# Four edits to the order of work in a two-layer backbone: a q tile's slot, gating written behind the next scores, a barrier behind a head's last scores, and spread roots in other PSUM banks

## The chip, the cores and the metric

The program runs on one core of one Trainium2 chip. The metric is the device time of one execution in microseconds (us), taken over several runs; lower is better. The core has five engines that each work through their own queue in order: TensorE (PE, matmuls; its weight loads are listed apart as PEld), VectorE (DVE), ScalarE (ACT), GpSimd (POOL) and SyncE (SP). In this kernel SP issues the loads from DRAM and POOL the stores to it.

## What is computed

Two layers over 512 latent tokens (x) and 256 context tokens, width 1024, batch 1. Layer 0 is a bidirectional multi-scale retention with 4 heads (q and k of 256 per head, v and a gate path z of 512 per head, rotary positions on q and k, a decay per head and direction); layer 1 is a chunked gMLP with a spatial gate. Each branch is gated by silu(z), projected, scaled by a gate from the conditioning vector, and added to x. Cut to what matters here:

```python
for i in range(DEPTH):                       # DEPTH = 2
    hx = rmsnorm(x, norm_g[i]) * (1 + scale_x) + shift_x
    hc = rmsnorm(ctx, norm_g[i]) * (1 + scale_c) + shift_c
    if i == 0:                               # retention, per head:
        s = (q @ k.T) * decay                # over context and latent keys, both directions
        o = s @ v
        o = o * rsqrt(mean(o * o) + eps)     # over the head's 512 columns
        out = (o * silu(z)) @ w_out
    else:                                    # gMLP
        u, v, z = hx @ w_in
        v = layernorm(v) * vnorm_g
        y = u * (w_s @ v_chunk + b_s)
        out = (y * silu(z)) @ w_out
    x = x + gate_x * out
return rmsnorm(x, final_g)
```

Everything is float32. The kernel writes each float32 operand of a matmul as a high and a low part and takes three products (low by high, high by low, high by high; `mm3`).

## The kernel before

**How an operand is split.** `split` casts on ScalarE (the high part) and subtracts on VectorE (the low part). Tiles that go through it appear in the profile under their names: `hl` (weights), `ph` and `pl` (scores), `qk`, `v`, `og` (the gated output of a head). Weights are first loaded as `raw` tiles.

**How weights are streamed.** `Stream` (`Q`) holds an ordered list of weight pieces. `pump` gives each load the first free slot of those it is allowed (w0 to w6 for the projections of layer 0) and `upto` makes the splits two pieces ahead of the product that uses them. Products over pairs of halves are arranged so that seven products do the work of eight: quads of raws 11, 12, 21, 22, with differences made on VectorE in place (`raw<-raw`). The last quad of layer 0's projections is `("vz", 3, 1)`, the one before it `("kq", 3)`.

**Layer 0.** The projections of all heads run first. Their results q, k (after `rope`), v and z go to DRAM through POOL and come back per head. `load_qk(h)` brings five tiles of a head (k, q, k, context k, q) into slots of SBUF and splits them; even and odd heads use different slots. `load_v(h)` does the same for v and z, `load_wo(h)` for the output weights, `decay(h)` for the head's decay table `dt`. These are generators: `aside` runs one step of one of them at a place written into the loops, and `step` runs one step of `background`, which reads the conditioning weights of the second layer (`ada_a` from `bg` tiles). The last of its four pieces uses the slots w2 and w3.

**A head, `attend`.** Six steps of scores (two halves of the queries, three pairs of key blocks). `score` makes the scores of a pair in a bank of the PSUM pool `tm` (two banks), multiplies them with the decay (`pf`, VectorE), and splits them (`ph` on ScalarE, `pl` on VectorE). `pv` multiplies scores with v two steps later (LAG = 2), into banks of the pool `ps` (six banks). After the last pair of a half `finish` takes the sums of squares and their root on ScalarE (`junk`, `ss`), the reciprocal on VectorE, and the gated rows `gt`; `flip` transposes them on TensorE and splits them into `og`. The flip of the first half stands at step 6 of the loop, between the P V products of scores 4 and 5 (counted from 0); the one of the second half inside the output projection, `project_out`.

**The turn to layer 1.** In the output projection of head 3 `prepare` starts the weight stream of layer 1 (`hl_e` is its first split, into a slot of its own), and the norm of the new x is taken: `by_tokens` transposes x into `ps` banks and sums squares, `inverse` makes the roots, `rms` spreads them over the partitions with four small matmuls into a PSUM bank and copies them to `rs`; `residual` copies the transposed x from its banks (`xs`). From `rs` follow the operands of layer 1, among them S1 (`oS`), which the third product, T1, needs.

**What sets the order.** TensorE's instructions keep the order of the text. On ScalarE, VectorE and the DMA queues a scheduler at build time may reorder, by data and by its own estimate of when things are ready, with text order as priority. The class `Queue` adds constraints: while `pinned` is set (inside `aside`), an instruction must follow the last one issued in the text on its engine; `kept` keeps all in order; `fence()` makes everything later in the text on that engine follow the last instruction issued before it:

```python
def fence(self):
    self.last = self.recent
```

A slot that is given out again is written only after its last reader. The functions that the change touches:

Of the kernel before, what the change touches and what calls it, by code (L numbers as in the profile page):

```python
# [10 lines left out]
ALU = mybir.AluOpType  # L11
AX = mybir.AxisListType

P = 128
# [12 lines left out]
HS = 256  # L27
# [40 lines left out]
def hybrid_kernel(ctx, tc, xT_d, cT_d, cv_d, sv_d, rows_d, ada0_d, adag_d, w_d, rope_d, dec_d, ws_d, id_d, out_d):  # L68
# [181 lines left out]
    for q in QUADS[3:]:  # L250
        Q.quad(q, SINGLE)
        for u in RAWS:
            Q.load((q, u), W, 1, parts_of(q, u))
    PROJECTED = len(Q.items)
    def place_at(tag):
        return lambda: st([P, 2, 1024], tag, F32R, name="hl_e")
# [506 lines left out]
    def background():  # L763
        for i in range(4):
            a = None
            for a in ada_piece(i, *(("g1", ("g2", "g3")) if i < 3 else ("oA22", ("w2", "w3")))):
                if a is None:
                    yield
            yield
            if i == 0:  # L770
                yield from columns(a, gate0)
                dve.tensor_tensor(gate0, gate0, gateb0, ALU.add)
            elif i == 1:
                yield from columns(a, sh1)
                dve.tensor_tensor(sh1, sh1, adab1[:, 0, :], ALU.add)
                dve.tensor_tensor(shs, sh1[:, 0:4], sh1[:, 4:8], ALU.add)
            elif i == 2:
                yield from columns(a, gs1)
                dve.tensor_tensor(gs1, gs1, adab1[:, 1, :], ALU.add)
                dve.scalar_tensor_tensor(gs1, gs1, 1.0, g1, ALU.add, ALU.mult)  # L780
            else:
                gb = st([P, D], "g1", name="gateb1")
                load(gb, rows_d[0:1, :].partition_broadcast(P))
                yield
                for j in range(2):
                    pr = pt(tag="tm")
                    mm(pr, ones, a[:, j * 512:j * 512 + 512], start=True, stop=True)
                    dve.tensor_tensor(gb[:, j * 512:j * 512 + 512], pr, gb[:, j * 512:j * 512 + 512], ALU.add)
                Q.gate = gb
            yield i  # L790
# [45 lines left out]
        dve.tensor_tensor(l, f32(l), f32(h), ALU.subtract)  # L836

    def load_qk(h):
        tags = ("s0", "s1", "s2", "s3", "rope") if h % 2 == 0 else ("w4", "w5", "g2", "g3", "w6")
        srcs = (k_d[h][0], q_d[h][0], k_d[h][1], kc_d[h], q_d[h][1])  # L840
        t = []
        for tag, src in zip(tags, srcs):
            t.append(st([P, 2, 2, HS], tag, F32R, name="qk"))
            load(f32(t[-1][:, 1]).rearrange("p a b -> p (a b)"), src)
            if len(t) % 2:
                yield
        for x in t:
            halves(x)
            yield
        qk[h] = (t[1], t[4]), (t[0], t[2]), t[3]  # L850
        yield
# [77 lines left out]
    def attend(h, qs, vs):  # L929
        q, k, kc = qk.pop(h)  # L930
        v, z = vv.pop(h)
        dt = dts[h]
        og = [st([P, 2, 4, HS], tag, F32R, name="og") for tag in ("oS3", "oS4")]
        steps = [(hf, j) for hf in range(2) for j in range(0, NK, 2)]
        ph, po, pend = {}, {}, []

        def key(j):
            return (k[j // 2], j % 2) if j < NT else (kc, j - NT)

        def score(hf, j):  # L940

            p = pt(tag="tm")
            for o in range(2):
                src, jj = key(j + 1 - o)
                for m in range(2):
                    l = (src[:, 0, m, jj * P:jj * P + P], src[:, 1, m, jj * P:jj * P + P])
                    mm3(p[:, o * HS:o * HS + HS], l, (q[hf][:, 0, m, :], q[hf][:, 1, m, :]), m == 0, m == 1)
            j1 = j + 1
            s0 = hf * HS - P * j1 + P * (NT - 1) if j < NT else XW + hf * HS - P * (j1 - NT) + P * (NC_T - 1)
            base = dt[:, s0:s0 + HS]  # L950
            both = bass.AP(base.tensor, base.offset, [base.ap[0], (P, 2), (1, HS)])
            two = lambda x: x.rearrange("p (o t) -> p o t", o=2)
            a = t2("pf")
            dve.scalar_tensor_tensor(two(a), two(p), 1.0 / 16.0, both, ALU.mult, ALU.mult)
            hl = t2("ph", dt=F32R), t2("pl", dt=F32R)
            split(hl, a)
            ph[hf, j] = hl

        def pv(hf, j):
            if j == 0:  # L960
                po[hf] = [pt(), pt()]
            h, l = ph.pop((hf, j))
            src = v[j // 2]
            for jj in range(2):
                for t in range(2):
                    o = (1 - jj) * HS + t * P
                    mm3(po[hf][t], (h[:, o:o + P], l[:, o:o + P]), (src[:, 0, jj, :], src[:, 1, jj, :]),
                        j + jj == 0, j + jj == NK - 1)
            if j == NK - 2:
                finish(hf)  # L970

        def finish(hf):
            ss = st([P, 2], "ss", bufs=2)
            for t in range(2):
                act.activation(t2("junk"), po[hf][t], AF.Square, accum_out=ss[:, t:t + 1])
            act.activation(ss, ss, AF.Sqrt, bias=eps, scale=1.0 / 512)
            dve.reciprocal(ss, ss)
            gts = []
            for t in range(2):
                g = t2("gt")  # L980
                dve.scalar_tensor_tensor(g, po[hf][t], ss[:, t:t + 1], z[:, 2 * hf + t, :], ALU.mult, ALU.mult)
                gts.append(g)
            pend.append((hf, gts))

        def flip():
            hf, gts = pend.pop(0)
            for fp in range(2):
                pq = pt()
                for b in range(2):
                    for t in range(2):  # L990
                        o = b * HS + t * P
                        pe.transpose(pq[:, o:o + P], gts[t][:, (2 * fp + b) * P:(2 * fp + b) * P + P], ident)
                src = pq.rearrange("p (b t) -> p b t", b=2)
                split((og[hf][:, 0, 2 * fp:2 * fp + 2, :], og[hf][:, 1, 2 * fp:2 * fp + 2, :]), src)

        LAG = 2
        wo = load_wo(h)
        for i in range(len(steps) + LAG):
            if i < len(steps):
                score(*steps[i])  # L1000
            if i >= LAG:
                pv(*steps[i - LAG])
            aside(qs)
            if i > 4:
                aside(vs)
            if i == len(steps):
                flip()
            if (h, i) == (0, 2):
                for c in range(4):
                    load(acc[:, 2 * c:2 * c + 2, :], xT_d[:, 2 * c:2 * c + 2, :])  # L1010
            if i < 5:
                aside(wo)
            if i in (3, 5, 6):
                step()
        return og, flip

    def project_out(ws, og, flip, parts, then=None, between=None, prepare=None):
# [72 lines left out]
        dve.reciprocal(s[:, 1, :], s[:, 1, :])  # L1090

    def rms(hf):
        pr = pt((P, HS))
        for i in range(2):
            mm(pr[:, i * P:i * P + P], sums[hf][:, 1, i:i + 1].to_broadcast([P, P]), ident, start=True, stop=True)
        rs = st([P, HS], "rs1", name="rs1")
# [324 lines left out]
```

## Time and profile before

| | |
|---|---|
| median of 3 runs | 913.14 us |
| runs | 909.51, 913.14, 913.16 us |
| the profiled execution's own time | 911.76 us |
| its span, first to last instruction | 910.0 us |
| TensorE busy | 886.6 us (97%) |
| VectorE busy | 722.4 us (79%) |
| ScalarE busy | 445.5 us (49%) |
| mean granted TensorE clock | 0.997 |

Nearly all instructions carry line 54 (the helper that issues them), so groups are told apart by the names of their tiles. In rows of the timeline the columns are: start, duration, engine, line, operation, output <- inputs, shapes, count, and in brackets the idle time of the engine before it with what ended it. In rows of stretches they are: the stretch, its length, the busy time of PE, PEld, DVE, ACT and POOL with their counts, the granted clock, the DMA engines' busy share, and GB/s.

In time, the projections of layer 0 reach to about 343 us, heads 0 to 3 follow at about 343, 395, 447 and 496 us (first scores), and the products of layer 1 begin near 554 us.

### The profile page before, as it was taken

The page shows a single profiled execution, that of the slowest core. Times are in us where ns is not written, and L with a number is a line of the kernel's source. Part 1 is how long each engine was busy: PE and PEld are TensorE (multiplying, and loading weights), DVE is VectorE, ACT ScalarE, POOL GpSimd, SP SyncE. Part 2 cuts the span into 40 slices and gives each one's busy share as a digit, 9 for nine tenths or more (in the row PEclk, how much of TensorE's full clock was granted, in tenths as well). Part 3 has the DMA queues.
Part 4 walks back from the last instruction along what each step waited for, and adds up shares of the span by engine and source line. Part 5 has one row for each costly group of instructions (what it writes and reads, how often), then busy time and mean ns, then how long its engine had stood idle before and what let it go on. Part 6 is the DMA issues. An engine that isn't in the chain of part 4 may idle for free.

```text
span 910.0 us, 16953 instructions
## 1 busy us (share of the span) xinstructions
PE 886.6 (97%) x6872; PEld 840.4 (92%) x6872; DVE 722.4 (79%) x1024; ACT 445.5 (49%) x683; POOL 51.5 (6%) x88
## 2 busy tenths in 40 slices
PE   8999999999999999999999999999999999999987
PEld 6899999999999998998989798999999899899885
DVE  3689978698789866888666759999899479679985
ACT  5565644434545436626362548744546445244244
POOL 0001211101102010000000001111000000000000
PEclk9999999999999999999999999999999999999999
DMA  9943968556667377758163611626335035037102
GB/s 334 389 136 111 308 200 255 163 183 223 211 207 241 107 254 251 257 164 282 43 194 107 200 37 66 200 102 220 129 116 185 24 116 185 24 117 253 49 24 93
DMA packets 76782, 153.81 MB, mean 169 GB/s; under 512 B 7840, under 2 KB 34592, under 8 KB 76704
## 3 DMA queue, kind: packets, MB, share of 16 engines
q1 hardware_dynamic: 69840, 130.70, 44.5%
q0 software_dynamic: 6720, 22.03, 6.3%
q8 instruction: 54, 0.88, 0.4%
q14 instruction: 24, 0.20, 0.1%
q10 hardware_dynamic: 144, 0.01, 0.0%
HBM read 128.58 MB, written 24.12 MB: 168 GB/s over the span
## 4 chain that ended last, share of the span: by engine, by line
PE 61%; DVE 20%; DMA 7%; ACT 5%; issue 5%; SPq 1%; DVEq 0%; ACTq 0%
PE pst L54 61%; DVE hl L54 5%; DMA raw<-in_w_dram 4%; DVE raw L54 4%; DVE ya L54 2%; ACT hl L54 2%; DVE o L54 2%; DMA vt<-vt 2%; SPq L128 1%; DMA acc<-in_xT_dram 1%; DVE pf L54 1%; DMA xq<-in_xT_dram 1%; DVE snap L54 1%; DVE ada_a L54 1%; ACT junk L54 1%
## 5 line engine op out<-in xcount | busy, mean ns | idle before, releaser
L54 DVE TENSOR_TENSOR hl<-raw,hl 128x1024 fp32r<-128x1024 f32 x195 | 236.7, 1222 | 65.5 <-ACT hl L54 64.8
L54 ACT CAST hl<-raw 128x1024 fp32r<-128x1024 f32 x195 | 202.7, 1049 | 140.9 <-DVE raw L54 71.1
L54 PE MATMUL pst<-oS,hl 128*128 128x256 f32 x1104 | 135.6, 280 | 4.3 <-DVE hl L54 3.7
L54 PEld LDWEIGHTS pst<-oS,hl 128*128 128x128 f32 x1104 | 131.4, 188 | 6.6 <-ACT ya L54 3.6
L54 PE MATMUL pst<-hl,oS 128*128 128x256 f32 x1152 | 137.3, 279 | 0.1
L54 PEld LDWEIGHTS pst<-hl,oS 128*128 128x128 f32 x1152 | 135.6, 188 | 1.2 <-ACT snap L54 0.8
L54 PE MATMUL pst<-oA,hl 128*128 128x256 f32 x936 | 118.1, 281 | 0.2
L54 PEld LDWEIGHTS pst<-oA,hl 128*128 128x128 f32 x936 | 112.6, 188 | 2.6 <-DVE raw L54 0.8
L54 DVE TENSOR_TENSOR raw<-raw 128x1024 f32<-128x1024 f32 x92 | 111.5, 1221 | 0.8
L54 PE MATMUL pst<-hl,oA 128*128 128x256 f32 x816 | 99.4, 280 | 0.1
L54 ACT COPY snap<-pst 128x512 f32<-128x512 f32 x92 | 53.9, 586 | 89.4 <-PE pst L54 89.1
L54 PEld LDWEIGHTS pst<-hl,oA 128*128 128x128 f32 x816 | 96.9, 188 | 0.4 <-issue 0.3
L54 PE MATMUL pst<-og,hl 128*128 128x256 f32 x768 | 93.1, 281 | 0.0
L54 PEld LDWEIGHTS pst<-og,hl 128*128 128x128 f32 x768 | 91.2, 188 | 1.0 <-issue 0.5
L54 PE MATMUL pst<-hl,ya 128*128 128x512 f32 x288 | 69.6, 394 | 2.4 <-DVE ya L54 2.4
L54 PEld LDWEIGHTS pst<-hl,ya 128*128 128x128 f32 x288 | 53.9, 188 | 14.7 <-DVE ya L54 2.9
L54 PE MATMUL pst<-v,ph 128*128 128x512 f32 x192 | 60.9, 399 | 0.0
L54 DVE TENSOR_TENSOR snap<-pst,snap 128x512 f32<-128x512 f32 x69 | 47.4, 687 | 4.1 <-PE pst L54 3.9
L54 ACT CAST ph<-pf 128x512 fp32r<-128x512 f32 x24 | 14.9, 621 | 70.9 <-DVE pf L54 68.5
L54 PE MATMUL pst<-hl,hc 128*128 128x256 f32 x384 | 47.5, 279 | 0.0
L54 PEld LDWEIGHTS pst<-hl,hc 128*128 128x128 f32 x384 | 45.9, 188 | 0.0
L54 PEld LDWEIGHTS pst<-v,ph 128*128 128x128 f32 x192 | 36.7, 191 | 7.7
(172 smaller groups left out, 971.8 us busy)
## 6 DMA issues: line engine op xcount, KB each, us to landing
raw<-in_w_dram SPq DMA_DIRECT2D x224, 256.0 KB, 4.5
bg<-in_adag_dram SPq DMA_DIRECT2D x32, 512.0 KB, 4.4
ada_w<-in_ada_dram SPq DMA_DIRECT2D x16, 512.0 KB, 9.0
raw<-in_w_dram SPq DMA_DIRECT2D x16, 512.0 KB, 4.4
bg<-in_dec_dram SPq DMA_DIRECT2D x12, 512.0 KB, 4.3
v<-snap POOLq DMA_DIRECT2D x16, 256.0 KB, 5.1
z<-snap POOLq DMA_DIRECT2D x16, 256.0 KB, 4.7
v<-v SPq DMA_DIRECT2D x8, 512.0 KB, 4.2
```

What stands on the lines that cost most here:

```text
L54: made = op(*args, **kw)
L128: nc.sync.dma_start(dst, src)
```

## The change

1. The second q tile of even heads is put into slot w3, not rope. So that w3 is free, the loads of the last projection quad may not use it, and the last background piece uses the slots w2 and rope.
2. `finish` stops after the root. Reciprocal and `gt` move to a new function `gated`, called behind the next `score` of the loop, and once behind the loop.
3. Behind the split of a head's last scores ScalarE and VectorE each get a `fence()`.
4. `rms` takes its bank from the pool `tm`, not `ps`.

```diff
-            Q.load((q, u), W, 1, parts_of(q, u))
+            Q.load((q, u), W if q != QUADS[-1] else [w for w in W if w != "w3"], 1, parts_of(q, u))
...
-            for a in ada_piece(i, *(("g1", ("g2", "g3")) if i < 3 else ("oA22", ("w2", "w3")))):
+            for a in ada_piece(i, *(("g1", ("g2", "g3")) if i < 3 else ("oA22", ("w2", "rope")))):
...
-        tags = ("s0", "s1", "s2", "s3", "rope") if h % 2 == 0 else ("w4", "w5", "g2", "g3", "w6")
+        tags = ("s0", "s1", "s2", "s3", "w3") if h % 2 == 0 else ("w4", "w5", "g2", "g3", "w6")
...
             split(hl, a)
+            if (hf, j) == steps[-1]:
+                act.fence()
+                dve.fence()
             ph[hf, j] = hl
...
             act.activation(ss, ss, AF.Sqrt, bias=eps, scale=1.0 / 512)
-            dve.reciprocal(ss, ss)
-            gts = []
-            for t in range(2):
-                g = t2("gt")
-                dve.scalar_tensor_tensor(g, po[hf][t], ss[:, t:t + 1], z[:, 2 * hf + t, :], ALU.mult, ALU.mult)
-                gts.append(g)
-            pend.append((hf, gts))
+            rest.append((hf, ss))
+
+        def gated():
+            while rest:
+                hf, ss = rest.pop(0)
+                dve.reciprocal(ss, ss)
+                gts = []
+                for t in range(2):
+                    g = t2("gt")
+                    dve.scalar_tensor_tensor(g, po[hf][t], ss[:, t:t + 1], z[:, 2 * hf + t, :], ALU.mult, ALU.mult)
+                    gts.append(g)
+                pend.append((hf, gts))
...
             if i < len(steps):
                 score(*steps[i])
+            gated()
             if i >= LAG:
                 pv(*steps[i - LAG])
...
+        gated()
         return og, flip
...
-        pr = pt((P, HS))
+        pr = pt((P, HS), tag="tm")
```

More of the change, by code (lines that the diff above doesn't have):

```diff
@@ L934, in attend @@
         steps = [(hf, j) for hf in range(2) for j in range(0, NK, 2)]
-        ph, po, pend = {}, {}, []
+        ph, po, pend, rest = {}, {}, [], []
         def key(j):
```

## The prediction

> **What bounds the kernel now.** The page first: TensorE is busy for 97% of the span, so a change of scheduling can only win where it stands still or runs slowly. Then the busy times by stretch around the edits, then the timeline of each place, which follows with its edit (of a timeline only the rows used are shown).
>
> ```profile
> PE 886.6 (97%) x6872; PEld 840.4 (92%) x6872; DVE 722.4 (79%) x1024; ACT 445.5 (49%) x683; POOL 51.5 (6%) x88
> ```
>
> The busy times by stretch:
>
> ```profile
> 520.00:530.00 10.00, 8.04 (x43) 7.10 (x44) 4.41 (x8) 4.10 (x9) 0.00 (x0) 0.83 0.16 52
> 530.00:550.00 20.00, 19.71 (x169) 19.23 (x167) 13.83 (x23) 10.96 (x26) 2.17 (x4) 1.00 0.15 54
> ...
> 560.00:610.00 50.00, 48.70 (x414) 48.25 (x413) 50.00 (x68) 31.71 (x45) 7.32 (x14) 1.00 0.46 153
> ```
>
> In the rows of stretches the second number is TensorE's busy time, then follow weight loads, VectorE, ScalarE, POOL, and the granted clock. From 520 to 530, in head 3, TensorE loses 1.96 us and has a clock of 0.83; in 560 to 610, the turn to layer 1, it loses 1.30 while VectorE is full for all 50 us. The other edits act at the start of head 0 and inside heads 0 to 2, shown below.
>
> **The q tile (w3 for rope).** The start of head 0:
>
> ```profile
> 314.86 2.96 PE L54 MATMUL pst<-oA,hl 128*128 128x256 f32 x24
> 335.07 0.68 DVE L54 TENSOR_TENSOR rope_b<-pst,rope 128x512 f32<-128x512 f32 x1
> 335.78 0.33 SPq L128 DMA_DIRECT2D qk<-q  x1
> 341.12 0.68 DVE L54 TENSOR_TENSOR snap<-pst,snap 128x512 f32<-128x512 f32 x1
> 343.10 2.99 PE L54 MATMUL pst<-qk 128*128 128x256 f32 x24
> 343.49 0.62 ACT L54 CAST qk<-qk 128x512 fp32r<-128x512 f32 x1 [3.54 <-DMA qk<-q]
> 346.75 0.69 DVE L54 SCALAR_TENSOR_TENSOR pf<-pst,dt 128x512 f32<-128x512 f32 x1
> 347.49 1.68 PE L54 MATMUL pst<-qk 128*128 128x256 f32 x12 [1.40 <-DVE pf L54]
> ```
>
> The load into rope goes out at 335.78, as soon as rope's last reader (335.07) ends, lands 7.7 us later among four loads of acc, and ScalarE stands 3.54 us before its cast. Behind that cast queue a Silu (its input is ready at 341.8), two casts of v, a copy and the first ph; VectorE's first pf comes at 346.75 although score 0 (half of the 24 matmuls) ended near 344.6, and the third score waits 1.40 us for that bank. In w3 the load needs only the release of raw 21 of quad (kq, 3), whose split is done before its T4 product at 314.86: about 20 us earlier. Without the wait the Silu runs at 341.9, the casts follow, pf starts near 344.75 and ends at 345.45, before score 1 ends at 346.09, so the third score follows at once. That is 1.40 us and the short wait for weights in front of it: **-1.5 us** (bounds 0, if ScalarE finds another late input, and -1.5). The same cast and subtraction lie in 318 to 340, beside dense matmuls.
>
> The rest of this edit costs nothing. Working `Stream.pump` through by hand, the last quad's loads take w1, w6, w2 and w0 already, so shutting w3 to them alters none. Background rows that went to w3 now go to rope, free at 335.8; piece 3 has its first reader two background steps later, in the loop of head 0, after 350. If such a load stands in SP's queue ahead of rope's release it holds z, a raw and acc back by at most 6 us; they are wanted from 350 on, ten us after.
>
> **Gating behind the scores, and the barrier, heads 0 to 2.** Head 1:
>
> ```profile
> 400.23 0.68 DVE L54 SCALAR_TENSOR_TENSOR pf<-pst,dt 128x512 f32<-128x512 f32 x1
> 400.83 1.22 DVE L54 TENSOR_TENSOR hl<-raw,hl 128x1024 fp32r<-128x1024 f32 x1
> 401.96 0.69 DVE L54 TENSOR_TENSOR pl<-pf,ph 128x512 fp32r<-128x512 f32 x1
> ...
> 409.98 1.57 PE L54 MATMUL pst<-qk 128*128 128x256 f32 x12
> 413.50 0.17 DVE L54 RECIPROCAL ss<-ss 128x2 f32<-128x2 f32 x1 [2.08 <-ACT ss L54]
> 413.70 1.41 DVE L54 SCALAR_TENSOR_TENSOR gt<-pst,ss,z 128x512 f32<-128x512 f32 x2
> 413.88 1.05 ACT L54 CAST hl<-raw 128x1024 fp32r<-128x1024 f32 x1
> 415.62 1.22 DVE L54 TENSOR_TENSOR hl<-raw,hl 128x1024 fp32r<-128x1024 f32 x1
> 416.76 0.68 DVE L54 SCALAR_TENSOR_TENSOR pf<-pst,dt 128x512 f32<-128x512 f32 x1
> 416.89 1.04 PE L54 MATMUL pst<-ident,gt 128*128 128x128 f32 x8
> 418.13 0.69 DVE L54 TENSOR_TENSOR pl<-pf,ph 128x512 fp32r<-128x512 f32 x1 [0.69 <-ACT ph L54]
> 418.88 0.50 PE L54 MATMUL pst<-v,pl 128*128 128x512 f32 x1 [0.95 <-DVE pl L54]
> ```
>
> Score 5 ends at 411.55 but its pf runs at 416.76, behind reciprocal, two gt, qk and hl; the last product of P and V waits 0.95 us for pl. Now pf goes into the 2.08 us gap (411.65 to 412.35). But reciprocal and gt must follow pl, and pl needs ph, which on ScalarE stands behind the casts of qk and hl, which are ahead in the text and ready when the root ends. So ph 414.9 to 415.5; VectorE: qk 414.0, hl 414.95 to 416.17, pl to 416.85, reciprocal, gt to 418.4. That an hl gets between pf and pl is the order of the first three rows. What is late next is the flip: TensorE reaches it at 416.89, in program order ahead of the last P V product, its second transpose waits for the second gt until 418.45, seven more take 0.9, and the P V product starts at 419.36 instead of 418.88: +0.48.
>
> Heads 0 and 2 have the same instructions in the same order, so I take the same there, +0.45 each. Together **+1.4 us**. The other bound is ph getting ahead of the hl cast: then gt is in time, and of the waits for pl the 0.95 of head 1 goes, -1.0. I take +1.4, since nothing in the text puts ph ahead. The gating of the second half, written after the loop, has four m-pairs of output projection (5.8 us) before its flip: nothing.
>
> **The barrier in head 3.**
>
> ```profile
> 511.58 1.57 PE L54 MATMUL pst<-qk 128*128 128x256 f32 x12
> 513.52 1.23 DVE L54 TENSOR_TENSOR hl_e<-raw,hl_e 128x1024 fp32r<-128x1024 f32 x1 [1.79 <-ACT hl_e L54]
> 514.79 2.48 DVE L54 TENSOR_TENSOR raw<-raw 128x1024 f32<-128x1024 f32 x2
> 518.49 1.34 PE L54 MATMUL pst<-ident,gt 128*128 128x128 f32 x8
> 521.96 0.50 PE L54 MATMUL pst<-v,pl 128*128 128x512 f32 x1 [2.12 <-DVE pl L54]
> ...
> 525.00:526.00 1.00, 1.00 (x4) 0.79 (x3) 0.00 (x0) 0.69 (x2) 0.00 (x0) 0.50 0.00 0
> 528.00 0.48 DVE L54 SCALAR_TENSOR_TENSOR acc<-pst,gate,acc 128x256 f32<-128x256 f32 x1 [4.90 <-PE pst L54]
> 882.83 17.44 PE L54 MATMUL pst<-hl,ya 128*128 128x512 f32 x75 [2.43 <-DVE ya L54]
> ```
>
> Here splits that the text has later (hl_e and two differences, 3.71 us of VectorE) came before the last scores, and the wait is 2.12 us. Behind the barrier they cannot. In head 1 the reciprocal starts 1.95 after score 5 ends; here score 5 ends at 513.15, so without hl_e's cast ahead of the squares the root is done by 514.6 to 515.1. I take 514.6: the last wo cast to 515.6, ph to 516.1; VectorE has pf at 513.3, hl to 516.9, pl to 517.5, both gt to 519.0. TensorE is at the flip at 518.4, waits 0.6 for the second gt, ends it near 519.95 and starts the P V product there: **-2.0 us**. After the old wait the clock fell to half: 0.83 over 10 us is 3.4 us at half rate, 1.7 us of full clock lost. With 0.6 us of waiting the clock should hold, as it did after the 0.95 in head 1: **-1.5 us**. Bounds for both: 0 and -3.6.
>
> What the barrier holds back is queued on VectorE and ScalarE behind pl and ph: hl_e, the two differences, the flip's og splits between them. The 3.71 us go into the 4.90 us in which VectorE waited before 528.00; TensorE first asks for og 2.9 us after the P V product starts, and hl_e and one difference fit before it. If that gap is gone, they come back in the full stretch behind 560, at up to 3.7. The raw slots that these splits free are freed later by as much, and SP's loads into them too; what TensorE then reads first was loaded before.
>
> The Trainium skill (TensorE: Matmul & The Clock Gate, Part 1) has the clock halved after an idle window of about 3.4 us, windows running free of the program, and restored after a busy one of that length. The 3.4 us of half rate agree; the wait of 2.12 us is shorter than its window, unless the transposes from 518.49 count as idle (3.47 us together), and after 2.43 us of waiting before 882.83 the 75 matmuls ran at full speed (0.233 us each). By that rule the loss at 523 is partly chance, and the sum without it -3.1.
>
> **Roots of the second norm in tm banks.**
>
> ```profile
> 560.20 0.16 DVE L54 RECIPROCAL sums<-sums 128x2 f32<-128x2 f32 x1
> 560.27 3.48 DVE L54 TENSOR_TENSOR raw<-raw 128x1024 f32<-128x1024 f32 x3
> 561.80 0.71 PE L54 MATMUL pst<-ident,sums 128*128 128x128 f32 x4 [1.16 <-ACT xs L54]
> 563.67 1.22 DVE L54 TENSOR_TENSOR f<-f,rs 128x1024 f32<-128x1024 f32 x1
> 568.26 16.91 PEld L54 LDWEIGHTS pst<-hl,oS 128*128 128x128 f32 x144 [0.34 <-DVE snap L54]
> ```
>
> The spread's operands exist at 560.36; it waits 1.16 us for a ps bank that ScalarE's xs copy frees. The tm banks are idle there, so it can run at 560.64. T1 at 568.26 needs S1, made from rs through f on VectorE, which is in the three differences; rs 1.1 us earlier lets f in after the second of them, 562.6 instead of 563.67, and T1 can start near 567.1: **-1.0 us**. Bounds -1.16 and 0 (f stays behind the third). The second B21 product needs the bank that rs is copied from; 2.9 us of the first cover that.
>
> **Sum.** -1.5 + 1.4 - 3.5 - 1.0 = -4.6 us. The profiled execution took 911.76, so 907.2; the median of the three runs, 913.14, lies 1.4 above it, so I forecast **908.5**. Bounds summed: -7.3 to +1.4.
>
> **Rivals.** (1) The flips are in time: ph ahead of the hl cast, -1.0 for +1.4, sum -7.0, **906.1**. For it: pf would be done 1.1 us before the root ends; against it: the casts stand first in the text. 0.18. (2) The other side: VectorE sets the pace from the barrier to 610. By the times above the barrier leaves it idle between the pl of score 4 and that of score 5 for 3.2 us (511.7, where the 1.79 before hl_e begins, to 516.8, less pf and hl) against those 1.79 now; if the gaps between 520 and 550 can't take the displaced work, the 1.4 us comes out at TensorE, head 3 and the roots win nothing, and the sum is -1.5 + 1.4 + 1.4 = +1.3, **914.4**. For it: VectorE full for 50 us; against: 5.6 and 6.2 us idle in the stretches of 520 to 550 above. It decides if less than 3.7 of these 11.8 us can be used. 0.16. (3) The half clock is not in every execution (the longer wait at 882 brought none; the lowest run is 3.6 below the median), so its removal shows little: -3.1, **910.0**. 0.14. (4) The edit of the q tile does not do what it says, ScalarE waiting for v or z instead of q: -3.1, **910.0** too. 0.10. The forecast itself has 0.42, with a range of its own from 907 to 910.
>
> **Chances.** About 0.5% (4.6 us) is what a measurement here tells from no change, and the forecast lies on that edge: a little over half of its 0.42, all of (1) and some luck of (3) make 0.45 for faster; the rest of it, (3), (4) and most of (2) make 0.47 for the same; a worse (2) 0.08 for slower. The range, 904.5 to 912.5, takes in (1) with a margin, (3), (4), and leaves out (2).
>
> **What would show it.** Right: no ScalarE wait for qk<-q near 340 and TensorE at 9.9 or more in that stretch; in each head pf of the last score before the reciprocal, and the wait moved from P V (for pl) to the transposes (for gt); hl_e after the last pl, clock 1.00 in 520 to 530; the spread at 560.6 of the old scale without a wait. Wrong: a wait for pl in head 3 above 1 us, a wait for hl or S1 after 560 that grows by what was won before, or transposes that wait more than 2 us.

## The result, and the profile after

| | before | after |
|---|---|---|
| median | 912.77 us (909.51 to 916.78, 15 runs) | 907.55 us (904.13 to 909.78, 15 runs) |
| ratio to before | | 0.9938, 95% interval 0.9924 to 0.9953 |
| the profiled execution's own time | 911.76 us | 908.74 us |
| its span | 910.0 us | 906.9 us |

The change makes the kernel 0.6% faster. The two profiled executions differ by 3.1 us in span, the medians by 5.2; the experiments say why.

The profile after, in the order of the prediction: first the busy line of the page, then the busy times by stretch (columns as before: stretch, length, PE, PEld, VectorE, ScalarE, POOL, granted clock, DMA share, GB/s).

```profile
PE 885.5 (98%) x6872; PEld 840.2 (93%) x6872; DVE 723.0 (80%) x1024; ACT 445.2 (49%) x683; POOL 51.5 (6%) x88
```

```profile
520.00:530.00 10.00, 10.00 (x79) 9.58 (x78) 8.45 (x14) 3.87 (x9) 0.00 (x0) 1.00 0.02 6
...
560.00:610.00 50.00, 48.97 (x418) 48.59 (x417) 49.91 (x68) 31.19 (x42) 5.94 (x11) 1.00 0.45 153
```

From 520 to 530 TensorE now works all 10 us (8.04 before) at a clock of 1.00 (0.83). From 560 to 610 it still misses 1.03 us and VectorE is still full.

The timeline of the changed kernel at the start of head 0, ScalarE, VectorE and TensorE:

```profile
341.78 0.63 ACT L54 ACTIVATE snap<-snap 128x512 f32<-128x512 f32 x1 [1.89 <-DVE snap L54]
...
344.59 0.69 DVE L54 SCALAR_TENSOR_TENSOR pf<-pst,dt 128x512 f32<-128x512 f32 x1
...
342.99 4.37 PE L54 MATMUL pst<-qk 128*128 128x256 f32 x36
347.19 0.39 PE L54 MATMUL pst<-v,pl 128*128 128x512 f32 x1
```

ScalarE no longer waits for the q load, the first pf starts at 344.59 (346.75 before), and the 36 products of three scores stand in one row without a wait. The first P V product comes at 347.19 in place of 349.23.

The end of the first half of head 1, VectorE and then TensorE:

```profile
410.42 0.69 DVE L54 SCALAR_TENSOR_TENSOR pf<-pst,dt 128x512 f32<-128x512 f32 x1
412.91 0.69 DVE L54 TENSOR_TENSOR qk<-qk 128x512 fp32r<-128x512 f32 x1 [1.80 <-ACT qk L54]
413.87 1.23 DVE L54 TENSOR_TENSOR hl<-raw,hl 128x1024 fp32r<-128x1024 f32 x1 [0.26 <-ACT hl L54]
415.01 0.68 DVE L54 TENSOR_TENSOR pl<-pf,ph 128x512 fp32r<-128x512 f32 x1
415.61 0.16 DVE L54 RECIPROCAL ss<-ss 128x2 f32<-128x2 f32 x1
415.80 1.41 DVE L54 SCALAR_TENSOR_TENSOR gt<-pst,ss,z 128x512 f32<-128x512 f32 x2
...
416.61 0.33 PE L54 MATMUL pst<-ident,gt 128*128 128x128 f32 x1 [0.71 <-DVE gt L54]
417.27 0.98 PE L54 MATMUL pst<-ident,gt 128*128 128x128 f32 x7 [0.33 <-DVE gt L54]
418.00 0.47 PE L54 MATMUL pst<-v,pl 128*128 128x512 f32 x1
```

This is the order that the prediction worked out: pf, qk, hl, pl, reciprocal, gt. The wait has moved from the P V product (for pl) to the transposes (for gt). In head 1 it comes to 1.04 us; the row of waits has five of them in the whole kernel:

```profile
PE pst L54 <- DVE gt L54: 1.8, 5, 0.7
```

Head 3 and the turn to layer 1, VectorE and then TensorE:

```profile
515.36 0.68 DVE L54 TENSOR_TENSOR pl<-pf,ph 128x512 fp32r<-128x512 f32 x1
515.97 0.16 DVE L54 RECIPROCAL ss<-ss 128x2 f32<-128x2 f32 x1
516.04 1.20 DVE L54 TENSOR_TENSOR hl_e<-raw,hl_e 128x1024 fp32r<-128x1024 f32 x1
517.16 1.40 DVE L54 SCALAR_TENSOR_TENSOR gt<-pst,ss,z 128x512 f32<-128x512 f32 x2
...
519.36 0.47 PE L54 MATMUL pst<-v,pl 128*128 128x512 f32 x1
...
522.19 5.77 PE L54 MATMUL pst<-og,hl 128*128 128x256 f32 x48
...
556.24 0.69 PE L54 MATMUL pst<-ident,sums 128*128 128x128 f32 x4
...
562.36 22.56 PE L54 MATMUL pst<-hl,oS 128*128 128x256 f32 x192
...
585.68 3.15 PE L54 MATMUL pst<-hl,oA 128*128 128x256 f32 x25 [0.75 <-DVE snap L54]
```

The last scores' pl is done before hl_e starts, so the P V product has nothing to wait for. The spread of the roots starts without a wait (before: 1.16 us), T1 comes 5.9 us earlier than before, and a new wait of 0.75 us for snap follows 23 us later.

The positions of TensorE's work in the two profiles give this ledger. It uses the start of the first scores of heads 0, 1 and 3, of the output projection behind head 3 (the first product of og and hl), of the first T1 product (hl,oS, near 565), and the end of the span:

| stage | before | after | difference | predicted |
|---|---|---|---|---|
| head 0 (first scores to those of head 1) | 51.56 | 49.58 | -1.98 | -1.5 + 0.45 |
| heads 1 and 2 | 101.60 | 102.86 | +1.26 | +0.93 |
| head 3, to the output projection | 30.03 | 26.76 | -3.27 | -3.5 |
| output projection to T1 | 41.97 | 40.17 | -1.80 | -1.0 |
| T1 to the end | 341.7 | 344.5 | +2.8 | 0 |

With the 0.1 us by which head 0 itself starts earlier, they add up to the -3.1 of the two spans. So the sum up to T1 was -5.9, and about half of that was lost again behind it.

### The profile page after: what moved, and what is told of

Same layout as the page of the kernel before. It is cut to its first block, busy times and chain, and to the rows that moved or that the text cites. A ratio compares the mean times of both kernels' runs of the same rounds, so it can differ in the third digit from the quotient of the medians.

```text
span 906.9 us, 16957 instructions
## 1 busy us (share of the span) xinstructions
PE 885.5 (98%) x6872; PEld 840.2 (93%) x6872; DVE 723.0 (80%) x1024; ACT 445.2 (49%) x683; POOL 51.5 (6%) x88
## 4 chain that ended last, share of the span: by engine, by line
PE 63%; DVE 19%; DMA 6%; ACT 6%; issue 5%; SPq 1%; DVEq 0%; ACTq 0%
PE pst L54 63%; DVE hl L54 5%; DVE raw L54 3%; DVE ya L54 3%; DMA vt<-vt 2%; ACT hl L54 2%; DMA raw<-in_w_dram 2%; DVE o L54 2%; ACT junk L54 1%; DMA xq<-in_xT_dram 1%; SPq L128 1%; DMA bg<-in_dec_dram 1%; DVE snap L54 1%; ACT L54 1%; DVE pl L54 1%
```

## The experiments

All stages of the ledger, read in the same way from the profile of every kernel (us; each is described below; "wait" is TensorE's wait for pf at the third score of head 0):

| kernel | wait | head 0 | heads 1, 2 | head 3 | to T1 | to the end | span | median of all its runs |
|---|---|---|---|---|---|---|---|---|
| before | 1.40 | 51.56 | 101.60 | 30.03 | 41.97 | 341.7 | 910.0 | 912.77 |
| barrier_alone | 2.34 | 53.49 | 101.39 | 25.88 | 41.87 | 345.6 | 911.1 | 910.04 |
| gating_alone | 1.26 | 51.27 | 102.21 | 28.09 | 41.87 | 342.9 | 909.7 | 911.42 |
| roots_alone | 2.52 | 52.52 | 101.43 | 28.41 | 40.17 | 344.7 | 910.5 | 910.82 |
| filled_wait | 3.64 | 54.70 | 101.28 | 28.74 | 41.91 | 341.1 | 910.9 | 913.12 |
| q_alone | 0 | 49.41 | 101.95 | 30.66 | 41.88 | 342.1 | 909.1 | 907.49 |
| q_barrier | 0 | 49.48 | 102.01 | 25.87 | 41.88 | 341.1 | 903.4 | 905.70 |
| all_but_gating | 0 | 49.38 | 101.14 | 25.87 | 40.19 | 344.9 | 904.3 | 903.58 |
| all_but_gating_again | 0 | 49.41 | 101.60 | 25.88 | 40.17 | 343.2 | 903.4 | 906.20 |
| after | 0 | 49.58 | 102.86 | 26.76 | 40.17 | 344.5 | 906.9 | 907.55 |
| after_again | 0 | 49.71 | 102.69 | 26.76 | 40.17 | 343.9 | 906.5 | 907.80 |
| wo_late | 0 | 49.16 | 100.05 | 25.88 | 40.18 | 342.8 | 901.1 | 902.99 |
| wo_late_again | 0 | 49.21 | 100.05 | 25.88 | 40.17 | 343.0 | 901.6 | 904.68 |
| wo_late_no_gating | 0 | 49.19 | 100.05 | 25.87 | 40.19 | 345.7 | 904.1 | 902.97 |

The medians come from four sets of runs, in which the kernel before had medians of 912.44 to 913.35 us. Where the same edits are in, the stage to T1 repeats to 0.1 us and heads 1 and 2 repeat to 0.9 us. Head 0 with the old slot (51.3 to 54.7), head 3 with neither the barrier nor the gating (28.4 to 30.7) and the tail (341.1 to 345.7) repeat worse: each has a wait behind which the clock fell in some profiles and not in others.

### One edit at a time

The q tile alone: the first part of the diff, the rest as before.

```diff
-            Q.load((q, u), W, 1, parts_of(q, u))
+            Q.load((q, u), W if q != QUADS[-1] else [w for w in W if w != "w3"], 1, parts_of(q, u))
...
-        tags = ("s0", "s1", "s2", "s3", "rope") if h % 2 == 0 else ("w4", "w5", "g2", "g3", "w6")
+        tags = ("s0", "s1", "s2", "s3", "w3") if h % 2 == 0 else ("w4", "w5", "g2", "g3", "w6")
```

> Only the q tile's edit (w3 for rope, and the slots that go with it) on the kernel before. Theory A (stages add up, but TensorE's gain is partly given back where a load sets the pace): no ScalarE wait for qk<-q near 340, first P V product of head 0 at 347.2 instead of 349.2 (-1.9 to -2.0); at the start of head 1 VectorE still waits for the background rows (bg), which are not earlier by as much, so the third scores wait 0.5 to 0.9 us for pf and head 2 begins only 1.0 to 1.3 early; wait for pl in head 3 and half clock as before. End: -1.0 us (-0.5 to -2.0), that is the ratio 0.998 to 0.9995. Rival B (the wait in head 1 belongs to the gating edit): no wait for pf in head 1, head 2 begins 1.9 early, -1.9 at the end.

Measured: 907.49 us, ratio 0.9946 (0.9925 to 0.9966), about as much as the whole change. Both theories expected far less (-1.0 and -1.9 us). In its profile the wait in head 0 is gone (head 0 49.41), and the stages behind follow rival B: no wait for pf in head 1, and head 2 starts 1.8 us earlier (445.07 for 446.88). The wait of 2.12 us and the half clock in head 3 are there as before. Why the median gains more than the 1.4 us of wait in the profile of before is seen in the other kernels that keep the old slot. The prediction shows ScalarE's cast of q in the kernel before, at 343.49 after a wait of 3.54 us. The same row from the timelines of barrier_alone, roots_alone and filled_wait, in this order, one fence each:

```profile
344.20 0.62 ACT L54 CAST qk<-qk 128x512 fp32r<-128x512 f32 x1 [4.48 <-DMA qk<-q]
```

```profile
344.75 0.62 ACT L54 CAST qk<-qk 128x512 fp32r<-128x512 f32 x1 [4.66 <-DMA qk<-q]
```

```profile
345.80 0.62 ACT L54 CAST qk<-qk 128x512 fp32r<-128x512 f32 x1 [5.79 <-DMA qk<-q]
```

No edit of these kernels acts before this place, yet the load among the transfers of acc lands at four different times, up to 2.3 us apart (gating_alone has 343.60 after 3.40 us), and TensorE's wait is between 1.26 and 3.64 us. Twice the clock fell after it too. Head 0 takes 52.7 us in the mean of the five executions with the old slot and 49.4 in the mean of the nine with w3: the edit is worth 3.3 us by these profiles, which the interval of the ratio (3.1 to 6.8 us) takes in, and it takes out a source of scatter. The profile of before had caught one of the smaller values. The clock has a share in it: the mean granted clock was 0.9955 over the 28 runs of the kernel before that were made beside q_alone, and 0.9979 over its own 11, and 0.0024 of 912 us are 2.2 us (an estimate).

The barrier alone:

```diff
             split(hl, a)
+            if (hf, j) == steps[-1]:
+                act.fence()
+                dve.fence()
             ph[hf, j] = hl
```

> Only the barrier on the kernel before; the gating stays ahead of the last scores. Theory A (the barrier is what wins head 3, since it keeps hl_e and two differences behind pl): heads 0 to 2 as before, 0.95 us of waiting for pl in head 1 stays; in head 3 pf follows the wo split, pl ends near 518.9 when the flip ends near 519.3, so the wait for pl goes from 2.12 to under 0.3, the clock stays 1.00 from 520 to 530, the output projection of head 3 begins near 522.2 instead of 526.29: -4.1 there, -3 to -4 at the end (ratio 0.9955 to 0.9965). Rival B (barrier only makes VectorE idle and the displaced 3.7 us come back behind 560): the projection begins 4 early, but waits for hl or S1 between 545 and 610 grow by 3 to 4, end within 1 us of before. Rival C (the gating is needed for it): wait for pl in head 3 stays above 1.5, clock still halved, 0.

Measured: 910.04 us, ratio 0.9969 (0.9949 to 0.9989). Head 3 falls from 30.03 to 25.88, all that can be had there: every kernel with the barrier and without the moved gating has 25.87 or 25.88 and no wait. That is the -4.1 of theory A; the time, -2.8 us by the ratio, is a little short of its -3 to -4. Rival C falls, and so does rival B: between 545 and 610 TensorE waits for the bank of the roots as before (1.16 us), and not for hl or S1. The profiled span (911.1) shows nothing of the gain, because this execution had 2.34 us of wait and a half clock in head 0 and the longest tail but one, with a half clock from 880.44 to 887.27.

The gating alone (`gated` as in the diff of the change, nothing else):

```diff
-            dve.reciprocal(ss, ss)
-            gts = []
...
+            rest.append((hf, ss))
...
                 score(*steps[i])
+            gated()
```

> Only the gating edit on the kernel before, no barrier. Theory A: pf of the last scores goes ahead of the reciprocal and the two gt come behind pl, so the wait for pl in head 1 (0.95) becomes a wait for gt at the transposes of 1.0 to 1.4; heads 0 and 2 +0.0 to +0.3; in head 3 hl_e and the differences still come before pl, the flip waits for gt about 3 us, P V near 521.9 as before, clock still halved after it. End 0 to +0.8 us. Rival C (the gating alone removes the waits): P V of head 3 1 to 2 us earlier, -1 to -3 at the end.

Measured: 911.42 us, ratio 0.9979 (0.9959 to 1.0), not clearly different from no change. By stages it costs 0.8 us in heads 1 and 2 over the mean of the other kernels with the old slot (102.21 to 101.4) and head 3 takes 28.09, where the wait of 2.12 us for pl gives way to waits for gt; the timeline of head 3:

```profile
520.66 0.33 PE L54 MATMUL pst<-ident,gt 128*128 128x128 f32 x1 [1.44 <-DVE gt L54]
521.32 0.98 PE L54 MATMUL pst<-ident,gt 128*128 128x128 f32 x7 [0.33 <-DVE gt L54]
```

The clock stayed at 1.00 here, against the expectation. Beside roots_alone, which has the old wait and the full clock too (28.41), the gating wins 0.3 us in head 3; most of the 1.9 us to the kernel before (30.03) is the clock.

### The change without the moved gating

The changed kernel with `gated` undone, measured twice; the second time beside the changed kernel once more.

```diff
-            rest.append((hf, ss))
+            dve.reciprocal(ss, ss)
+            gts = []
...
                 score(*steps[i])
-            gated()
```

> The changed kernel with the gating put back ahead of the next scores (q tile, barrier and roots stay). Theory A (the gating edit itself costs, since the second gt then comes behind pl): against the changed kernel the transposes no longer wait for gt (1.8 us in all there); waits for pl of about 0.1, 0.95 and 0.1 in heads 0 to 2 come back, head 3 has no wait at all; 0.5 to 1.0 us faster than the changed kernel, about -5.5 to -6.5 against the kernel before (ratio 0.993 to 0.994). Rival C (gating and barrier only work together): waits for pl of 1 to 2 us in head 3, slower than the changed kernel by 1 to 3 us.

> The changed kernel itself, beside the three variants below, so that they are compared on one chip. Both theories: a ratio to the kernel before between 0.992 and 0.996 (it was 0.9938), waits of TensorE for gt near 1.8 us in all and one wait for pf near 0.7 us at the start of head 1.

> The change without the moved gating. Theory A: the moved gating costs what its waits say. In heads 0 to 2 the gated halves come behind pf, qk, hl and pl, so the second half's transposes wait (gt 1.8 us in all), and the earlier ph cast of ScalarE lets loads start earlier, which delay the decay background by 1.1 us and with it head 1's first pf (0.7 us). Without it 2.0 to 3.0 us less than the changed kernel, no wait for gt and none for pf. Rival B: the time from 560 on is set by VectorE, which is full there, so what is won in the heads is lost in waits for snap and hl: within 0.8 us of the changed kernel.

Measured: 903.58 us, ratio 0.9902 (0.9877 to 0.9927), then 906.20, 0.9929 (0.9914 to 0.9943), beside 907.80, 0.994 (0.9926 to 0.9954), for the changed kernel. Each time this one is the faster; the size is not settled by the medians, since 907.80 - 906.20 = 1.6 us is within the two intervals. The profiles settle it better: 1.1 to 1.7 us in heads 1 and 2 (0.7 to 0.9 against q_alone and q_barrier, which have the new slot and no moved gating either), 0.9 in head 3, 3.1 of span in the second pair and 2.6 in the first. That is near the 2.0 to 3.0 of the second expectation; the 0.5 to 1.0 of the first was too little. Head 3 has no wait for pl, so rival C falls. Rival B, that VectorE's full stretch gives the gain back, falls by the stages: to T1 and to the end the two kernels take the same within the scatter of the tail. So the moved gating, which the prediction priced at +1.4 in heads 0 to 2, costs 2 to 2.5 us in all four (0.2 to 0.3 in head 0, then 1.1 to 1.4 in the mean, then 0.9).

### The roots of the second norm

Alone, and undone in the kernel without the moved gating (q_barrier):

```diff
-        pr = pt((P, HS))
+        pr = pt((P, HS), tag="tm")
```

The kernel of q_barrier differs from what its name says in one more line. `spread`, which does for the first norm and the decay, ahead of head 0, what `rms` does here, takes its bank from `ps` there:

```diff
     def spread(s, name):
 
-        pr = pt((P, HS), tag="tm")
+        pr = pt((P, HS))
```

Nothing of that shows in its stages: head 0 starts at 343.05 us, in the other kernels at 342.78 to 343.35.

> The kernel before, with only the spread roots in other banks. Theory A: the spread starts 1.3 us earlier after the output projection and the first T1 product (hl,oS) 1.6 us earlier, TensorE then waits 0.7 us for snap, VectorE is full from 570 to 625, and the end is within 0.8 us of the kernel before. Rival: the 1.6 us arrive at the end. In both, the wait for the old q slot at the start of head 0 stays (pf between 1.2 and 2.4 us).

> The change without the moved gating and without the other banks for the spread roots. Against all_but_gating it gives what the roots are worth. Theory A (won at 556 to 562, given back by the waits for snap at 585 and for hl at 589 and 690): within 0.7 us of all_but_gating, and its wait for snap is gone. Rival (the 1.65 us that the spread starts earlier arrive at the end): 1.3 to 2.0 us more than all_but_gating.

Measured: roots_alone 910.82 us, ratio 0.9991 (0.9961 to 1.0022); q_barrier 905.70 us, 0.9925 (0.9906 to 0.9944), beside 906.20 for all_but_gating_again. The roots are worth nothing that can be measured, as theory A had it. The intervals are too wide to exclude the rival's 1.6 us by the times alone, so the stages have to decide. The eight kernels with the edit reach T1 in 40.17 to 40.19 us, the six without in 41.87 to 41.97: 1.7 won. From the first product of T1 to the next long run of hl,oS (near 600) the six need 39.45 to 39.69 us and the eight 40.73 to 40.87: 1.2 lost again within 40 us. The timeline of TensorE in all_but_gating shows where:

```profile
582.67 3.16 PE L54 MATMUL pst<-hl,oA 128*128 128x256 f32 x25 [0.75 <-DVE snap L54]
586.11 14.15 PE L54 MATMUL pst<-hl,oA 128*128 128x256 f32 x119 [0.28 <-DVE hl L54]
```

The same two waits, 0.74 or 0.75 and 0.26 to 0.29 us, stand in all eight and in none of the six. VectorE is full there: in all_but_gating it is busy for 53.80 us of the 55 from 570 to 625 (the third busy time of this row of stretches):

```profile
570.00:625.00 55.00, 53.98 (x461) 53.60 (x460) 53.80 (x70) 28.02 (x34) 6.12 (x12) 1.00 0.58 194
```

### What stood ahead of the gate: the last split of wo

In head 1 above, the late gt comes behind an hl of 1.23 us. It belongs to a split of the head's output weights that the loop takes in step 4. Moved to step 6 in the changed kernel (wo_late, wo_late_again), and in the changed kernel without the moved gating (wo_late_no_gating):

```diff
-            if i < 5:
+            if i in (0, 1, 2, 3, 6):
                 aside(wo)
```

> The changed kernel with the last of the five splits of wo taken behind the gated halves (loop step 6 in place of 4), so that hl no longer stands ahead of the reciprocal on VectorE. Theory A: gt comes 1.1 us earlier, the waits for gt fall from 1.8 to under 0.5 us, the wait for pf at head 1 (another mechanism) stays near 0.7 us; 1.0 to 1.8 us less than the changed kernel. Rival: the split is late for the output projection, or VectorE's total holds the heads, and the time is within 0.5 us of the changed kernel.

> The changed kernel with the last split of wo behind the gated halves, once more, beside the same without the moved gating. Both theories: 3 to 6 us less than the changed kernel's 907.6, no wait for gt, none for pf.

> The changed kernel without the moved gating, and with the last split of wo at loop step 6. Theory A: the moved gating pays once hl is out of its way, because pf and the next scores come before the gate; the late split by itself is worth under 0.5 us. Head 3 then starts near 493.5 to 494.3, as in all_but_gating, and the time is 1.5 to 3 us above wo_late_again. Rival B: the place of the split is what pays, the moved gating gives nothing; head 3 starts near 492.2 and the time is within 0.8 us of wo_late_again.

Measured: 902.99 us, ratio 0.9888 (0.9869 to 0.9907); again 904.68, 0.9924 (0.9896 to 0.9951); without the moved gating 902.97, 0.9913 (0.9885 to 0.994). The repetition is 2.9 us below the 907.6, just short of the 3 to 6 expected. In wo_late no wait for gt, pl or pf is left in the four heads. The timeline of head 1, VectorE and TensorE:

```profile
411.34 0.69 DVE L54 TENSOR_TENSOR qk<-qk 128x512 fp32r<-128x512 f32 x1 [1.53 <-ACT qk L54]
411.95 0.68 DVE L54 TENSOR_TENSOR pl<-pf,ph 128x512 fp32r<-128x512 f32 x1
412.56 0.15 DVE L54 RECIPROCAL ss<-ss 128x2 f32<-128x2 f32 x1
412.75 1.41 DVE L54 SCALAR_TENSOR_TENSOR gt<-pst,ss,z 128x512 f32<-128x512 f32 x2
...
414.43 1.03 PE L54 MATMUL pst<-ident,gt 128*128 128x128 f32 x8
415.22 0.48 PE L54 MATMUL pst<-v,pl 128*128 128x512 f32 x1
```

The second gt ends at 414.16 and the eight transposes run in one piece from 414.43. Theory A named the mechanism but undersized it: it put the gain at 1.0 to 1.8 us, and the stages show 0.4 + 2.8 + 0.9 = 4.1 us (49.58, 102.86 and 26.76 less 49.16, 100.05 and 25.88), the medians measured side by side 907.80 - 902.99 = 4.8. Part of the surplus is the wait for pf at the start of head 1, which I had put down to loads that collide and expected to stay. In the changed kernel VectorE has this row there:

```profile
391.48 1.28 DVE L54 SCALAR_TENSOR_TENSOR ada_a<-bg,cpad,ada_a 128x1024 f32<-128x1024 f32 x1 [2.25 <-DMA bg<-in_adag_dram]
```

In wo_late the wait for this load is 0.79 us and that for pf is gone, although ScalarE waits longer than before for a decay row (5.13 us for bg<-in_dec, 4.61 in the changed kernel). So the account by collisions does not hold as I gave it; why the background row comes earlier relative to VectorE's work was not tried by itself.

Against expectation, the moved gating gives nothing once hl is out of the way: with and without it heads 1 and 2 take 100.05 us, and the medians are 902.97 without, 904.68 with. Theory A of wo_late_no_gating falls, its rival stands: head 3 starts at 492.33 us (theory A 493.5 to 494.3, the rival 492.2), and the place of the split is what pays. The medians differ by 1.7 us, more than the rival's 0.8, but within the two intervals. With these kernels the version without the moved gating and with the split at step 6 is at least as fast as any, 8 to 10 us (about 1%) below the kernel before, and 2.3 (by the ratios) to 4.6 (by the medians) below the change.

### The half clock in head 3

Ten products of ones, written to a bank that nothing reads, behind the transposes of head 3's flip in the kernel before:

```diff
             if i == len(steps):
                 flip()
+                if h == HEADS - 1:
+                    filled = pt(tag="tm")
+                    for _ in range(10):
+                        mm(filled[:, :P], ones, ones, start=True, stop=True, skip_group_check=True)
```

> The kernel before, with ten 128x128 products of ones (into a bank that nothing reads) put behind the transposes of head 3's last flip, in front of the last P V products. Theory A: the half clock at 525 comes from TensorE doing nothing there for 2.1 us; the ten products fill a part, the clock stays 1.00 from 520 to 530, the output projection starts at the same distance from head 3's start less 1.2 to 1.6 us (28.4 to 28.8 in place of 30.0). Rival B: it comes from a stretch without products of the usual kind, transposes included, that the ten do not break up, or of the wait's end: clock 0.83, distance 30.0 or more.

Measured: 913.12 us, ratio 1.0017 (0.9999 to 1.0036). Head 3 takes 28.74 us, the range that theory A gave, with a clock of 1.00. Yet the run does not tell the theories apart, because another kernel without the filling has the same: roots_alone leaves head 3 untouched, has the same wait of 2.12 us, and a clock of 1.00. Its timeline and stretch, and the stretch of q_alone, which has the wait as well:

```profile
522.73 0.50 PE L54 MATMUL pst<-v,pl 128*128 128x512 f32 x1 [2.12 <-DVE pl L54]
```

```profile
520.00:530.00 10.00, 7.88 (x56) 7.12 (x55) 5.99 (x10) 4.10 (x9) 0.00 (x0) 1.00 0.18 52
```

```profile
520.00:530.00 10.00, 9.33 (x54) 8.38 (x55) 5.09 (x9) 3.37 (x8) 0.00 (x0) 0.83 0.17 52
```

Two executions with this wait (before, q_alone) lost the clock and needed 30.03 and 30.66 us for head 3, the third (roots_alone) kept it and needed 28.41. The half clock is thus worth about 1.6 us where it strikes (30.03 less 28.41; q_alone has a wait of 0.33 us for gt on top), and it does not always strike.

The profiles show when it does. In each of the 14 the clock changes only at times that lie whole periods of 3.41 us apart: in the kernel before it is full for 152 such periods, half for one, full for 112. The periods around the wait in head 3, of before and then of roots_alone:

```profile
519.69:523.11 3.42, 1.29 (x7) 0.98 (x6) 2.73 (x5) 1.59 (x3) 0.00 (x0) 1.00 0.28 89
523.11:526.52 3.41, 3.41 (x11) 2.63 (x10) 0.00 (x0) 0.69 (x2) 0.00 (x0) 0.50 0.19 65
```

```profile
517.88:521.29 3.41, 2.72 (x16) 1.96 (x14) 3.37 (x6) 0.10 (x1) 0.00 (x0) 1.00 0.37 124
521.29:524.71 3.42, 1.98 (x9) 1.64 (x10) 1.90 (x4) 1.59 (x3) 0.00 (x0) 1.00 0.51 149
524.71:528.12 3.41, 3.41 (x27) 3.24 (x26) 0.92 (x3) 2.51 (x6) 0.00 (x0) 1.00 0.01 5
```

In before the whole wait falls into one period; TensorE works for 1.29 us of it, and the next period runs at half clock. In roots_alone a boundary at 521.29 cuts the same wait in two, 2.72 and 1.98 us of work are left, and the clock holds. Over all 14 profiles the clock fell 13 times while TensorE had work left, each time behind a period with 0.11 to 1.49 us of work, and it stayed full behind every period with 1.57 us or more. Transposes count as work in this: in all_but_gating_again the period 12.10 to 15.51 holds 2.19 us of transposes and nothing else, and the clock stayed full.

By these profiles theory A is right that missing work is the cause, and rival B is wrong to count the transposes as missing. The filling could not tell: without its products the two periods that they fall into (520.11 to 523.53 and 523.53 to 526.94, 3.17 and 3.41 us of work) would have kept at least 2.4 and 1.8 us by estimate, so the clock would have held in that execution without them too. The bound between 1.49 and 1.57 us is read from these profiles after the fact; no run was made to test it. The Trainium skill (TensorE: Matmul & The Clock Gate, Part 1) has windows of about 3.4 us that run free of the program, and the half clock after an idle one. The traces agree on the length and on the running free, and here a window with up to 1.49 us of work counted as idle.

## Why the prediction came out

The forecast was 908.5 us and the result 907.55, inside its range, with its main terms in place. Point by point:

- **The q tile (-1.5).** Right in mechanism: the wait for the load goes, Silu, casts and pf move up by the times worked out (Silu 341.9 forecast and 341.78 found, pf 344.75 and 344.59). Mis-sized: the pair of profiles gives about -2.0, and the means of the table -3.3 (52.7 to 49.4). The step that failed was to read a late transfer's wait from one execution as its price, with -1.5 as the lower bound. This and the tail, below, are the two largest parts of the difference between the pair of spans (-3.1) and the medians (-5.2).
- **The flips of heads 0 to 2 (+1.4).** Right in order, and in sum partly by luck: +1.26 in heads 1 and 2 against 0.93, about +0.2 in head 0 (49.58 to 49.41 in q_alone) against 0.45. One part was too dear: the remaining transposes were given 0.9 us to the P V product, and 0.73 passed (417.27 to 418.00). One was not seen, and it is half of the 1.26: the wait for pf of 0.66 us at the start of head 1 (0.36 in after_again).
- **Head 3 (-3.5).** Measured -3.27. The barrier alone gives -4.15 in these profiles, the moved gating takes 0.88 back (the prediction had 0.6 for that wait within its sum). The clock term, -1.5, was there in this pair, but it is not in every execution: rival (3) named that, and roots_alone bears it out: it depends on where the boundary of a period falls in the wait. The transposes, which the prediction thought might count as idle, do not. In the mean of the three executions with the wait of 2.12 us head 3 takes 29.7, so the typical gain is 2.9.
- **The roots (-1.0).** The gain up to T1 was larger, -1.7: f followed after one of the three differences, where the forecast had two ahead of it (VectorE's rows below). But what mattered was the next step, and the prediction's sum had none: TensorE's next wait, for snap from a full VectorE, takes 1.2 of it back within 40 us (with the one for hl behind it). A wait behind 560 that grows by what was won before is one of the prediction's own signs of being wrong, and here it came. At the end nothing is left that can be measured. The prediction asked of rival (2) whether VectorE would limit the stretch behind 560, and did not put the same question to its own term.

VectorE in the changed kernel, where before three differences stood ahead of f:

```profile
556.00 0.16 DVE L54 RECIPROCAL sums<-sums 128x2 f32<-128x2 f32 x1
556.07 1.20 DVE L54 TENSOR_TENSOR raw<-raw 128x1024 f32<-128x1024 f32 x1
557.36 1.23 DVE L54 TENSOR_TENSOR f<-f,rs 128x1024 f32<-128x1024 f32 x1
```

- **The tail.** The pair lost 2.8 us behind T1, for which the sum had no term. Of these 1.3 are the waits after the roots. For the rest a half clock is enough that the profile of before does not have (3.41 us at half rate are 1.7 us lost). In the changed kernel a wait of 2.33 us for hl ends at 683.09 and leaves 1.08 us of work in its period; in the kernel before the wait at this place is 1.60 us, the period has 2.08 us of work, and the clock stays full. The changed kernel:

```profile
680.24:683.65 3.41, 1.08 (x10) 0.91 (x9) 3.31 (x5) 3.01 (x5) 0.00 (x0) 1.00 0.00 0
683.65:687.07 3.42, 3.42 (x19) 3.42 (x18) 3.40 (x3) 2.37 (x3) 0.00 (x0) 0.50 0.06 8
```

  The same chance makes part of the scatter of the 14 tails (341.1 to 345.7): nine have a half clock while TensorE had work left. all_but_gating, which has one behind 876.71, and its repetition, which has none, differ by 1.7 us.
- **Rivals.** (1), flips in time, did not happen in this change; the wo_late kernels reach the state it describes, ph ahead of the hl cast, by moving that cast, and it is worth more than its price there: 4.1 us in the stages, where -7.0 against -4.6 meant 2.4. (2) is true for the roots alone, not for the heads. (4) falls with q_alone.

Put together with the means of these profiles, which is an estimate: -3.1 (head 0, from 52.7 to the 49.6 of the two profiles of the changed kernel), +1.4 (heads 1 and 2), -2.9 (head 3), -1.7 (to T1) and +1.7 (the mean tail of the eight kernels with the roots moved, 344.1, less that of the six others, 342.4) make -4.6 us, near the -5.2 of the medians. That the forecast's -4.6 came so close is luck in two of its terms: an undersized q tile and a roots term that was given back offset each other.

## What to carry to other kernels

The wait for one transfer issued among four larger ones varied here from 3.40 to 5.79 us; one profile gives one draw of it, so price its removal by several profiles, or by a range reaching well above the one seen. When a result comes too late for its reader, look first at the work that an in-order engine takes just ahead of it: here moving one background split of 1.2 us by two loop steps gave 4.1 us, and made the rewritten gating needless. And for each microsecond won ahead of a stretch in which another engine is full, look for the next wait on that engine before counting it.

## What the hardware showed

The granted clock does not follow the length of the wait ahead of it. After waits of 2.34 and 3.64 us at the start of head 0 it fell, after one of 2.52 us it did not. What it follows in these profiles is TensorE's work in periods of 3.41 us whose place has nothing to do with the program. The periods around the waits of 2.34 us (barrier_alone) and 2.52 us (roots_alone):

```profile
344.55:347.96 3.41, 1.31 (x12) 1.10 (x10) 2.33 (x3) 3.16 (x5) 1.35 (x2) 1.00 0.98 395
347.96:351.38 3.42, 3.18 (x14) 3.09 (x15) 2.69 (x5) 1.44 (x3) 0.00 (x0) 0.50 0.29 111
```

```profile
343.79:347.21 3.42, 2.44 (x21) 2.24 (x19) 1.03 (x2) 2.46 (x4) 0.67 (x1) 1.00 1.03 414
347.21:350.62 3.41, 1.81 (x13) 1.60 (x14) 3.41 (x5) 1.68 (x3) 0.68 (x1) 1.00 0.63 246
350.62:354.04 3.42, 3.42 (x18) 2.92 (x19) 2.69 (x4) 2.48 (x4) 0.00 (x0) 1.00 0.31 80
```

TensorE's busy time is the second number and the clock the first behind the groups in brackets. The wait for ya near 880 shows the same at one and the same length: it is 2.18 us long in five of the profiles, and behind it the clock fell in three (after_again, wo_late, wo_late_no_gating) and held in two (gating_alone, q_barrier).

And a single load, issued at the same place of the program among four of 512 KB, kept ScalarE waiting for 3.40 to 5.79 us in the five executions with the old slot.
